# A hybrid attention and mLSTM step: the fourth head's scan on the projection's PSUM banks, run three blocks ahead, and a small DMA scratch

## The chip, the cores and the metric

The kernel runs on one core of one Trainium2 chip. The metric is the time of one execution on the device, in microseconds (us). Before the change, three runs gave 1586.22, 1588.04 and 1590.58 us; their median is 1588.04 us. The profile is one further execution, recorded by the hardware.

The engines are named as in the profile: PE is TensorE (matmuls), PEld its weight loads, DVE is VectorE, ACT is ScalarE, POOL is GpSimd, and SP is the engine that starts most DMAs. Each engine works through its own instructions strictly in the order of its queue. `L137` is line 137 of the kernel's source.

## The reference

One layer of a transformer-like step for 128 context tokens and 1024 latent tokens, D = 1024. Attention heads and mLSTM heads read one input projection and share one output projection, and a SwiGLU FFN follows. In short:

```python
h = rmsnorm(x, norm1_w) * (1 + sc1) + sh1                # sh1 .. g2 come from silu(cond) @ w_ada
aq, ak, av, mq, mk, mv, mo, mg = split(h @ w_in)
aq, ak = rope(rmsnorm(aq, q_norm_w)), rope(rmsnorm(ak, k_norm_w))   # rotary on latent tokens only
attn_o = softmax(aq @ keys.T / 8) @ vals                 # 8 query heads of 64, 2 key heads
hm = mlstm_bidir(mq, mk / sqrt(128), mv, gates)          # 4 heads of 128, forward and backward
hm = rmsnorm(hm) * sigmoid(mo)
x = x + g1 * (concat(attn_o, hm) @ w_out)
h2 = rmsnorm(x, norm2_w) * (1 + sc2) + sh2
x = x + g2 * swiglu(h2, w_gu, w_down)
# mlstm_scan, for one chunk of 128 tokens:
log_d = where(mask, b[:, None] - b[None, :] + i[None, :], -inf)
s = (q @ k.T) * exp(log_d - m_t)
num = s @ v + inter * (q @ C)                            # C, n: the state before this chunk
den = s.sum(-1) + inter * (q @ n)
out = num / maximum(abs(den), exp(-m_t))
```

The outputs are the two token groups after the layer, the normed keys and values of the context tokens, and the context's final mLSTM states.

## The kernel before

The tokens are nine blocks of 128 (block 0 is the context), in three chunks of three blocks. The program is one large function. Python generators emit pieces of the different strands of work in turns (`weave`, `beside`, `chain`), and a scheduler of the framework then sets the order of each engine's queue from the order of emission, from priorities (`hot`) and from its own model of when operands and memory are ready. Tiles are taken from pools; a tile whose memory was used by another must wait until the last use of that one. So both the number of buffers and the place of a pool in memory shape the order.

The stages by time in the profile:

- 0 to 84 us: the modulation of the inputs (`features`, L500 to L511, which makes `full` on DVE in pool `p0`) and the projection for keys, values and gates.
- 84 to 185 us: the projection of the queries (`linear_tok`, groups of blocks (0,1), (2,3), (4), (5,6), (7,8)). Beside it run the gates' work (L600 to L655), part of the modulation's matmuls with `w_ada` (`ada_rest`, L423 and L341), and the norm and rotary embedding (`norm_rope`, L657 to L686): first of the keys, in three calls, then of each query group after its evacuation (L724). One such call is: square on ACT (L664), sum on DVE (L666), a reciprocal root in twelve small DVE instructions (L127 to L133), a product on POOL (L668), the rotary products on DVE (L679) and POOL (L685), the sum on DVE (L686). Its scratch tile `nr` has one buffer, so the calls pass one behind another. `kw`, `qw`, and the tables `cc` and `ss` for keys and for queries are loaded at L913 to L922 into pool `qp`.
- 185 to 469 us: heads 0 to 3 of the mLSTM. `head_project` (L739) projects a head and forms its states; `head_mlstm` (L821), the scan, runs one head behind. Attention's first chunk runs beside both. The pairs of weights of a head are made on ACT and DVE (L198, L218, L219, L222, L137) from `iraw`, which SP loads (L193).
- 469 to 536 us: the scan of the fourth head, with no projection left, interleaved with the last modulation piece (`ada`, two buffers), the first half of the output projection (`attn_out_first`, L1144 to L1146) and attention's second chunk.
- 536 to 600 us: the second half of the output projection, and the second norm. Then the FFN to the end.

In the scan, `weights(b)` makes for a block the product of queries and keys and the masked log weights in one PSUM bank `pd` (PE, L840 to L843), two exponentials `dt` (ACT, L846), and their product `sd` (DVE, L848). For each block the scan then forms `pm` (PE L863, queries by states), `it` (ACT L866), `pn` (PE L870, `sd` by values), `nu` (DVE L873 or L875) and, after the normaliser, `hm` (ACT L883, DVE L884), the outputs of the head, which are stored to `hm_d` when several blocks are complete (L895). Before, `weights` runs one block ahead. `pd`, `pm`, `pn`, the modulation's and output projection's tiles and attention's transposes all take turns in the three banks of `bank()` (tag "mm"); two more banks (tag "wi", `bankA()`) belong to the projection and lie idle while the fourth head is scanned, and three hold attention's scores.

Of the kernel before, what the change touches and what calls it, by code (L numbers as in the profile page):

```python
# [8 lines left out]
F32 = mybir.dt.float32  # L9
F32R = mybir.dt.float32r  # L10
F16 = mybir.dt.float16
BF16 = mybir.dt.bfloat16
# [7 lines left out]
P = 128  # L20
D = 1024
KD = D // P
NB = 9
# [5 lines left out]
NH = 4  # L29
# [11 lines left out]
CSB = 21  # L41
# [4 lines left out]
def hybrid_step(ctx: ExitStack, tc: tile.TileContext, I: dict, O: dict):  # L46
    nc = tc.nc
# [10 lines left out]
    def nm(s):  # L58
        uid[0] += 1
        return f"{s}_{uid[0]}"  # L60
# [42 lines left out]
    def bank():  # L103
        return psum["mm"].tile([P, 512], F32, name=nm("mm"), tag="mm")
# [13 lines left out]
    def bc(ap, axis, shape):  # L118
        return ap.unsqueeze(axis).to_broadcast(shape)

    def rsqrt(tp, ss, n, inv, cap=16, plus=EPS):

        v = tp.tile([P, cap], F32, name=nm("rv"), tag="rv", bufs=2)[:, :n]
        y = tp.tile([P, cap], F32, name=nm("ry"), tag="ry", bufs=2)[:, :n]
        t = tp.tile([P, cap], F32, name=nm("rt"), tag="rt", bufs=2)[:, :n]
        h = tp.tile([P, cap], I32, name=nm("rh"), tag="rh", bufs=2)[:, :n]
        dve.tensor_scalar(out=v, in0=ss, scalar1=inv, scalar2=plus, op0=ALU.mult, op1=ALU.add)  # L127
        dve.tensor_scalar(out=h, in0=v.bitcast(I32), scalar1=1, scalar2=None, op0=ALU.logical_shift_right)
        dve.tensor_scalar(out=y.bitcast(I32), in0=h, scalar1=-1, scalar2=0x5F3759DF, op0=ALU.mult, op1=ALU.add)
        for _ in range(3):  # L130
            dve.tensor_tensor(out=t, in0=y, in1=y, op=ALU.mult)
            dve.scalar_tensor_tensor(out=t, in0=t, scalar=-0.5, in1=v, op0=ALU.mult, op1=ALU.mult)
            dve.scalar_tensor_tensor(out=y, in0=t, scalar=1.5, in1=y, op0=ALU.add, op1=ALU.mult)  # L133
        return y
# [389 lines left out]
    es0.close()  # L524
    mlp = es1.enter_context(tc.tile_pool(name="mlp", bufs=1, reuse_waits="tile"))
    mwh = mlp.tile([P, 512], F32, name="mwh")
    for tag, shape, bufs, dt in (("cs", [P, P + 1], CSB, F32), ("c0f", [P, P + 1], 2, F32), ("c0b", [P, P + 1], 1, F32), ("hm", [P, NB, P], 1, F32), ("ssh", [P, NB], 1, F32), ("nu", [P, 2, P + 1], 2, F32),
                                 ("it", [P, 2, P + 1], 1, F32), ("dn", [P, 2], 3, F32), ("jkh", [P, P], 1, BF16), ("sd", [P, 2, P], 2, F32),
                                 ("dt", [P, 2, P], 2, F32), ("so", [P, P], 9, F32), ("va", [P, P + 1], 9, F32), ("kT", [P, P], 9, F32),
                                 ("th", [P, P], 1, F32), ("qTm", [P, CT], 2 * NCH, F32), ("wv", [P, 2, P + 1], 2, F32), ("kt", [P, P], 2, F32)):  # L530
        mlp.tile(shape, dt, name=f"lay_{tag}", tag=tag, bufs=bufs)

# [204 lines left out]
    def qcol(i, d, b, h):  # L737
        c = d * 64 + b * 4 + h
        return QT[:, i, c : c + 1]  # L739
# [85 lines left out]
    def head_mlstm(h, st):  # L825

        blocks, states = st["b"], st["s"]
        for b in range(NBL, 1, -1):
            col = 64 + b * 4 + h
            dve.scalar_tensor_tensor(out=st["raw"][b], in0=states[1, b], scalar=decb[:, col : col + 1], in1=st["raw"][b],  # L830
                                     op0=ALU.mult, op1=ALU.add)
            states[1, b - 1] = st["raw"][b]
        hm = mlp.tile([P, NB, P], F32, name=nm("hm"), tag="hm", bufs=1)
        ssh = mlp.tile([P, NB], F32, name=nm("ssh"), tag="ssh", bufs=1)
        ends = {2: 0, 5: 3, 8: 6} if h == NH - 1 else {8: 0}

        def weights(b):
            qTb = st["q"][b // CB][:, b % CB * P : (b % CB + 1) * P]
            pd = bank()
            mm(pd[:, 0:P], blocks[b][0], qTb, start=True, stop=True)  # L840
# [3 lines left out]
            dt = mlp.tile([P, 2, P], F32, name=nm("dt"), tag="dt", bufs=2)  # L844
            for d in range(2):
                act(dt[:, d], pd[:, (d + 1) * P : (d + 2) * P], AF.Exp, bias=qcol(0, d, b, h))  # L846
            sd = mlp.tile([P, 2, P], F32, name=nm("sd"), tag="sd", bufs=2)
            dve.tensor_tensor(out=sd, in0=bc(pd[:, 0:P], 1, [P, 2, P]), in1=dt, op=ALU.mult)  # L848
            return qTb, sd

        ahead = [weights(0)]
        yield
        for b in range(NB):
            qTb, sd = ahead.pop(0)
            _, va, so = blocks[b]
            nu = mlp.tile([P, 2, P + 1], F32, name=nm("nu"), tag="nu", bufs=2)
            if b + 1 < NB:
                ahead.append(weights(b + 1))
            yield
            if b > 0:  # L860
                pm = bank()
                for d in range(2):
                    mm(pm[:, d * 256 : d * 256 + P + 1], qTb, states[d, b], start=True, stop=True)  # L863
                it = mlp.tile([P, 2, P + 1], F32, name=nm("it"), tag="it", bufs=1)
                for d in range(2):
                    act(it[:, d], pm[:, d * 256 : d * 256 + P + 1], AF.Copy, scale=qcol(2, d, b, h))  # L866
            yield
            pn = bank()
            for d in range(2):
                mm(pn[:, d * 256 : d * 256 + P + 1], sd[:, d], va, start=True, stop=True)  # L870
# [12 lines left out]
            act(hm[:, b, :], nu[:, 0, 0:P], AF.Copy, scale=dn[:, 0:1])  # L883
# [12 lines left out]
            yield  # L896
# [648 lines left out]
```

## Time and profile before

| | |
|---|---|
| runs, median of 3 | 1588.04 us (1586.22 to 1590.58) |
| the profiled execution, span | 1590.3 us |
| PE busy in it | 1494.7 us (94%) |
| DVE, ACT, POOL busy | 1027.2, 768.8, 267.4 us |
| PE busy, 125 to 185 us | 48.72 of 60 us |
| PE busy, 469 to 536 us | 52.78 of 67 us |
| PE busy, 600 to 1590 us | 969.91 of 990 us |

The profiled execution is one of its own, 2.3 us above the median of the runs. An engine's busy time says how much it does; what sets the end is read from the waits: for each wait of PE the profile names the instruction that ended it. Such a view is an inference from semaphores, and a wait for two things is put down to the later one. PEclk is the share of the full clock that TensorE was granted in a stretch.

### The profile page before, as it was taken

How to read it: one execution, taken by the hardware profiler on the slowest of the kernel's cores; microseconds unless marked ns; L12 is line 12 of the kernel's file. 1: busy time of each engine (PE TensorE's matmuls, PEld its weight loads, DVE VectorE, ACT ScalarE, POOL GpSimd, SP SyncE). 2: the span in 40 equal slices, each digit the busy share in tenths (PEclk: the TensorE clock that was granted, in tenths of full speed). 3: DMA queues.
4: the chain of work that ended last, by engine and by line, in shares of the span. 5: the costliest groups of instructions: out<-in, count | busy, mean ns of one | idle time of the engine just before them, and what ended most of it. 6: DMA issues, size and time to landing. Idle time of an engine off the chain costs nothing.

```text
span 1590.3 us, 23425 instructions
## 1 busy us (share of the span) xinstructions
PE 1494.7 (94%) x8539; PEld 1249.4 (79%) x8539; DVE 1027.2 (65%) x2025; ACT 768.8 (48%) x1409; POOL 267.4 (17%) x357
## 2 busy tenths in 40 slices
PE   6799799999988679999999999999999999999996
PEld 3544467666766467888999999999898989999995
DVE  4778645755757576667654667877875575554555
ACT  4854365846656354535433435555552443323332
POOL 0023342332332243100110001000010101001111
PEclk9899899999999899999999999999999999999998
DMA  9474322432547746957754547968774445544441
GB/s 358 160 200 140 94 75 36 103 77 52 117 113 179 237 103 149 221 158 176 173 158 129 159 127 230 198 154 198 165 173 126 153 133 178 155 121 137 146 144 53
DMA packets 387881, 236.91 MB, mean 149 GB/s; under 512 B 170198, under 2 KB 346790, under 8 KB 387766
## 3 DMA queue, kind: packets, MB, share of 16 engines
q1 hardware_dynamic: 385110, 231.84, 54.0%
q10 hardware_dynamic: 2656, 3.58, 1.1%
q8 instruction: 67, 1.10, 0.3%
q14 instruction: 48, 0.39, 0.1%
HBM read 183.79 MB, written 13.26 MB: 124 GB/s over the span
## 4 chain that ended last, share of the span: by engine, by line
PE 75%; DVE 9%; DMA 8%; ACT 4%; issue 2%; SPq 1%; POOL 1%; ACTq 0%; DVEq 0%; POOLq 0%
PE mm L1313 11%; PE mm L1314 11%; PE mm L1312 11%; PE mm L1112 5%; PE mm L1113 5%; PE mm L1114 5%; PE S L1032 4%; PE wi L485 3%; PE wi L483 3%; PE wi L484 3%; PE mm L1144 1%; PE mm L1145 1%; DMA aw<-in_w_ada_dram 1%; PE po L1057 1%; PE po L1056 1%
## 5 line engine op out<-in xcount | busy, mean ns | idle before, releaser
L152 ACT CAST whi<-raw 128x1024 fp32r<-128x1024 f32 (+1 forms) x216 | 221.8, 1027 | 413.0 <-PE mm L1313 151.5
L137 DVE TENSOR_TENSOR wlo<-raw,whi 128x1024 fp32r<-128x1024 f32 (+1 forms) x216 | 260.5, 1206 | 203.8 <-ACT whi L152 203.2
L1313 PE MATMUL mm<-aTl,whi 128*128 128x384 f32 x1056 | 355.9, 337 | 2.7 <-DVE aTl L137 2.7
L1314 PE MATMUL mm<-aTh,wlo 128*128 128x384 f32 x1056 | 354.3, 335 | 0.0
L1312 PE MATMUL mm<-aTh,whi 128*128 128x384 f32 x1056 | 353.2, 336 | 0.0
L137 POOL TENSOR_TENSOR hl<-tn,hl 128x384 fp32r<-128x384 f32 x66 | 85.5, 1295 | 839.5 <-ACT hl L1335 721.3
L1313 PEld LDWEIGHTS mm<-aTl,whi 128*128 128x128 f32 x1056 | 198.5, 188 | 3.9 <-DVE aTl L137 3.3
L1312 PEld LDWEIGHTS mm<-aTh,whi 128*128 128x128 f32 x1056 | 198.1, 188 | 0.6
L1314 PEld LDWEIGHTS mm<-aTh,wlo 128*128 128x128 f32 x1056 | 198.4, 188 | 0.0
L1113 PE MATMUL mm<-wlo,hl 128*128 128x512 f32 x372 | 145.5, 392 | 0.0
L1112 PE MATMUL mm<-whi,hl 128*128 128x512 f32 x372 | 144.1, 392 | 0.0
L1114 PE MATMUL mm<-whi,hl 128*128 128x512 f32 x372 | 143.2, 392 | 0.0
L483 PE MATMUL wi<-ipair,hT 128*128 128x384 f16 (+2 forms) x408 | 136.2, 337 | 1.8 <-ACT hT L507 1.2
L484 PE MATMUL wi<-ipair,hT 128*128 128x384 f16 (+2 forms) x408 | 136.4, 337 | 0.0
L485 PE MATMUL wi<-ipair,hT 128*128 128x384 f16 (+2 forms) x408 | 132.5, 337 | 1.0 <-DVE hT L137 1.0
L1039 DVE SCALAR_TENSOR_TENSOR pl<-pr,st,ph 128x1152 f16<-128x1152 f32 (+1 forms) x72 | 93.8, 1303 | 33.8 <-ACT ph L1038 33.7
L1034 DVE TENSOR_REDUCE st<-S 128x1 f32<-128x1152 f32 (+1 forms) x72 | 88.9, 1235 | 14.6 <-PE S L1032 14.1
L1032 PE MATMUL S<-kst,qT 128*128 128x384 f32 (+1 forms) x400 | 87.6, 350 | 9.8 <-ACT pr L1035 5.6
L1035 ACT ACTIVATE pr<-S,st 128x1152 f32<-128x1152 f32 (+1 forms) x72 | 81.3, 1129 | 29.6 <-DVE st L1034 25.6
L1038 ACT ACTIVATE ph<-pr,st 128x1152 f16<-128x1152 f32 (+1 forms) x72 | 83.8, 1165 | 23.2 <-DVE st L1037 6.7
L1101 DVE TENSOR_TENSOR t<-mm,gl 128x512 f32<-128x512 f32 x102 | 68.9, 685 | 28.1 <-DMA gl<-g_d 10.2
L1032 PEld LDWEIGHTS S<-kst,qT 128*128 128x128 f32 x400 | 70.6, 191 | 14.7 <-ACT pr L1035 7.0
(366 smaller groups left out, 2539.7 us busy)
## 6 DMA issues: line engine op xcount, KB each, us to landing
raw<-in_w_gu_dram SPq DMA_DIRECT2D x132, 512.0 KB
raw<-in_w_down_dram SPq DMA_DIRECT2D x60, 512.0 KB
a<-in_w_ada_dram SPq DMA_DIRECT2D x24, 512.0 KB
gl<-g_d SPq DMA_DIRECT2D x36, 256.0 KB
aw<-in_w_ada_dram SPq DMA_DIRECT2D x16, 512.0 KB
iraw<-in_w_in_dram SPq DMA_DIRECT2D x32, 256.0 KB
raw<-in_w_out_dram SPq DMA_DIRECT2D x12, 512.0 KB
x<-in_x_sample_dram SPq DMA_DIRECT2D x11, 512.0 KB
```

The source lines that it names most:

```text
L137: (dve if eng == "dve" else pool).tensor_tensor(out=out, in0=full, in1=hi, op=ALU.subtract)
L152: nc.scalar.copy(hi[:, :n], raw[:, :n])
L483: mm(ps[:, :n], ah, wh[:, k % 2, c0 : c0 + n], start=(k == 0), stop=False)
L484: mm(ps[:, :n], ah, wl[:, k % 2, c0 : c0 + n], start=False, stop=False)
L485: mm(ps[:, :n], al, wh[:, k % 2, c0 : c0 + n], start=False, stop=(k == KD - 1))
L1032: mm(S[:, n, 0:w], qT[:, h, :], kst[kv][:, t, c0 + n * w : c0 + (n + 1) * w], start=(t == 0), stop=(t == 1))
L1112: mm(ps, ah, wh[:, k % 2, :], start=(k == 0), stop=False)
L1113: mm(ps, ah, wl[:, k % 2, :], start=False, stop=False)
L1114: mm(ps, al, wh[:, k % 2, :], start=False, stop=(k == nk - 1))
L1312: mm(ps, wh[:, k, :], th[:, k, :], start=(k == 0), stop=False)
L1313: mm(ps, wh[:, k, :], tl[:, k, :], start=False, stop=False)
L1314: mm(ps, wl[:, k, :], th[:, k, :], start=False, stop=(k == KD - 1))
```

## The change

Three things, all in the diff:

1. In the scan of the fourth head alone (`alone`), `pm` and `pn` are taken from the projection's two banks (`wide = bankA`), and `weights` runs three blocks ahead in place of one (`depth = 3`).
2. More buffers for all heads: `hm` and `ssh` two in place of one, `nu` four for two, `it` three for one, `sd` and `dt` four for two. Together these are some 12.9 KB more in each partition.
3. The scratch that the program sets aside for dynamic DMAs, at the lowest addresses of each partition, is 256 bytes in place of 16384. All pools lie lower by the difference.

```diff
-    ... ("hm", [P, NB, P], 1, F32), ("ssh", [P, NB], 1, F32), ("nu", [P, 2, P + 1], 2, F32),
-        ("it", [P, 2, P + 1], 1, F32), ..., ("sd", [P, 2, P], 2, F32), ("dt", [P, 2, P], 2, F32), ...
+    ... ("hm", [P, NB, P], 2, F32), ("ssh", [P, NB], 2, F32), ("nu", [P, 2, P + 1], 4, F32),
+        ("it", [P, 2, P + 1], 3, F32), ..., ("sd", [P, 2, P], 4, F32), ("dt", [P, 2, P], 4, F32), ...
...
-        ends = {2: 0, 5: 3, 8: 6} if h == NH - 1 else {8: 0}
+        alone = h == NH - 1
+        ends = {2: 0, 5: 3, 8: 6} if alone else {8: 0}
+        depth = 3 if alone else 1
+        wide = bankA if alone else bank
...
-        ahead = [weights(0)]
+        ahead = [weights(b) for b in range(depth)]
...
-            if b + 1 < NB:
-                ahead.append(weights(b + 1))
+            if b + depth < NB:
+                ahead.append(weights(b + depth))
...
-                pm = bank()
+                pm = wide()
...
-            pn = bank()
+            pn = wide()
...
-    nc = _bacc.Bacc("TRN2", target_bir_lowering=False, num_devices=1)
+    nc = _bacc.Bacc("TRN2", target_bir_lowering=False, num_devices=1, dynamic_dma_scratch_size=256)
```

The lines of the changed kernel are three further down from L836 on (L913 before is L916 now).

What this does to the order of the queues is seen at three places. First SP, the engine that starts the DMAs, during the first projection. Before, `row` is the last load of that strand, and the keys' and queries' norm weights and rotary tables come behind all the later loads and stores of that strand:

```order
L448 DMA row_932<-in_b_ada_dram 2x512
L695 DMA out_new_cache_v_dram<-vall 128x128
L423 DMA a_93_784<-in_w_ada_dram 128x4x256
...
L193 DMA iraw_1059<-in_w_in_dram 128x4x128 x2
L734 DMA mwh<-in_mlstm_norm_w_dram 128x512
L913 DMA kw<-in_k_norm_w_dram 128x64
L914 DMA qw<-in_q_norm_w_dram 128x64
L921 DMA cc_1028<-in_k_cos_dram 128x8x64
L922 DMA ss_1029<-in_k_sin_dram 128x8x64
L921 DMA cc_1035<-in_k_cos_dram 128x8x64
L922 DMA ss_1036<-in_k_sin_dram 128x8x64
```

Now:

```order
L448 DMA row_932<-in_b_ada_dram 2x512
L916 DMA kw<-in_k_norm_w_dram 128x64
L917 DMA qw<-in_q_norm_w_dram 128x64
L924 DMA cc_1028<-in_k_cos_dram 128x8x64
L925 DMA ss_1029<-in_k_sin_dram 128x8x64
L924 DMA cc_1035<-in_k_cos_dram 128x8x64
L925 DMA ss_1036<-in_k_sin_dram 128x8x64
L695 DMA out_new_cache_v_dram<-vall 128x128
L423 DMA a_93_784<-in_w_ada_dram 128x4x256
```

The six loads moved up past the store of the context's values and all the later loads of `w_ada`.

Second DVE, at the end of the query projection, where the weight pairs of head 0 (`ipair`) are made and attention's first queries (`qT`) are formed. `nr_213` and `qraw_1606` are the third query group, block (4); `nrs_1759` and `nr_230` are the fourth, blocks (5, 6). Before:

```order
L137 TENSOR_TENSOR ipair_1902<-iraw_1062,ipair_1902 128x1024
...
L679 TENSOR_TENSOR nr_213_1629<-qraw_1606,ss_1036 128x16x16 x2
...
L686 TENSOR_TENSOR qraw_1606<-qraw_1606,nr_213_1629 128x512
L666 TENSOR_REDUCE nrs_1759<-nr_224_1757 128x16
...
L137 TENSOR_TENSOR qT_1986<-mm_1987,qT_1986 64x4x128
...
L137 TENSOR_TENSOR qT_1986<-mm_1987,qT_1986 64x4x128
L679 TENSOR_TENSOR nr_230_1778<-qraw_1754,ss_1036 128x16x16 x4
```

Now:

```order
L679 TENSOR_TENSOR nr_213_1629<-qraw_1606,ss_1036 128x16x16 x2
L219 TENSOR_SCALAR ipair_1892<-iraw_1059,isc_1211,ipair_1892 128x1024
L686 TENSOR_TENSOR qraw_1606<-qraw_1606,nr_213_1629 128x512
L137 TENSOR_TENSOR ipair_1895<-iraw_1060,ipair_1895 128x1024
L666 TENSOR_REDUCE nrs_1759<-nr_224_1757 128x16
...
L137 TENSOR_TENSOR ipair_1902<-iraw_1062,ipair_1902 128x1024
L137 TENSOR_TENSOR qT_1986<-mm_1987,qT_1986 64x4x128
L679 TENSOR_TENSOR nr_230_1778<-qraw_1754,ss_1036 128x16x16 x4
L137 TENSOR_TENSOR qT_1986<-mm_1987,qT_1986 64x4x128
```

The query groups' norm stands more than a group further up against the making of the pairs, and the second `qT` is now behind the fourth group's rotary product.

Third PE, at the start of the fourth head's scan (`pd` is a group of three matmuls; `ip` is a piece of `w_ada`). Before:

```order
L843 MATMUL mm_5728<-NM_105,selb 128x256
L840 MATMUL mm_5738<-qT_4749,kT_5074 128x128
...
L843 MATMUL mm_5738<-NM_105,selb 128x256
L870 MATMUL mm_5757<-va_4967,sd_5735 128x129 x2
L341 MATMUL mm_5765<-ip_5712,gta 32x256 x4
L341 MATMUL mm_5765<-ip_5711,gta 32x256 x4
L840 MATMUL mm_5776<-qT_4749,kT_5168 128x128
```

Now:

```order
L846 MATMUL mm_5728<-NM_105,selb 128x256
L843 MATMUL mm_5737<-qT_4749,kT_5074 128x128
...
L846 MATMUL mm_5737<-NM_105,selb 128x256
L843 MATMUL mm_5746<-qT_4749,kT_5168 128x128
...
L846 MATMUL mm_5746<-NM_105,selb 128x256
L843 MATMUL mm_5756<-qT_4820,kT_5260 128x128
...
L846 MATMUL mm_5756<-NM_105,selb 128x256
L873 MATMUL wi_5775<-va_4967,sd_5735 128x129 x2
L866 MATMUL wi_5807<-c_904_4690,qT_4749 128x129
L341 MATMUL mm_5783<-ip_5712,gta 32x256 x4
```

Four groups of weights stand ahead of the first product with the values, in place of two, and that product is in a bank of the projection (`wi`).

More of the change, by code (lines that the diff above doesn't have):

```diff
@@ L526, in hybrid_step @@
     mwh = mlp.tile([P, 512], F32, name="mwh")
-    for tag, shape, bufs, dt in (("cs", [P, P + 1], CSB, F32), ("c0f", [P, P + 1], 2, F32), ("c0b", [P, P + 1], 1, F32), ("hm", [P, NB, P], 1, F32), ("ssh", [P, NB], 1, F32), ("nu", [P, 2, P + 1], 2, F32),
-                                 ("it", [P, 2, P + 1], 1, F32), ("dn", [P, 2], 3, F32), ("jkh", [P, P], 1, BF16), ("sd", [P, 2, P], 2, F32),
-                                 ("dt", [P, 2, P], 2, F32), ("so", [P, P], 9, F32), ("va", [P, P + 1], 9, F32), ("kT", [P, P], 9, F32),
+    for tag, shape, bufs, dt in (("cs", [P, P + 1], CSB, F32), ("c0f", [P, P + 1], 2, F32), ("c0b", [P, P + 1], 1, F32), ("hm", [P, NB, P], 2, F32), ("ssh", [P, NB], 2, F32), ("nu", [P, 2, P + 1], 4, F32),
+                                 ("it", [P, 2, P + 1], 3, F32), ("dn", [P, 2], 3, F32), ("jkh", [P, P], 1, BF16), ("sd", [P, 2, P], 4, F32),
+                                 ("dt", [P, 2, P], 4, F32), ("so", [P, P], 9, F32), ("va", [P, P + 1], 9, F32), ("kT", [P, P], 9, F32),
                                  ("th", [P, P], 1, F32), ("qTm", [P, CT], 2 * NCH, F32), ("wv", [P, 2, P + 1], 2, F32), ("kt", [P, P], 2, F32)):
@@ L832, in head_mlstm @@
             states[1, b - 1] = st["raw"][b]
-        hm = mlp.tile([P, NB, P], F32, name=nm("hm"), tag="hm", bufs=1)
-        ssh = mlp.tile([P, NB], F32, name=nm("ssh"), tag="ssh", bufs=1)
-        ends = {2: 0, 5: 3, 8: 6} if h == NH - 1 else {8: 0}
+        hm = mlp.tile([P, NB, P], F32, name=nm("hm"), tag="hm", bufs=2)
+        ssh = mlp.tile([P, NB], F32, name=nm("ssh"), tag="ssh", bufs=2)
+        alone = h == NH - 1
+        ends = {2: 0, 5: 3, 8: 6} if alone else {8: 0}
+        depth = 3 if alone else 1
+        wide = bankA if alone else bank
         def weights(b):
```

8 lines of the change are left out of this document (4 added, 4 removed).

## The prediction

> **What bounds the kernel now.** I read the page's head first, then the busy times by stretch, then TensorE's waits inside the two stretches that the change touches, and last the chain of waits there. The head of the page:
>
> ```profile
> span 1590.3 us, 23425 instructions
> PE 1494.7 (94%) x8539; PEld 1249.4 (79%) x8539; DVE 1027.2 (65%) x2025; ACT 768.8 (48%) x1409; POOL 267.4 (17%) x357
> ```
>
> TensorE (PE) is busy 94% of the span, so a gain must come from the 95.6 us in which it is not, or from its clock. The windows show where those lie. Their columns are: stretch, length, busy time (with counts) of PE, its weight loads, DVE, ACT and POOL, then the granted clock, DMA share and GB/s.
>
> ```profile
> 50.00:70.00 20.00, 18.66 (x154) 14.65 (x152) 18.32 (x60) 16.27 (x42) 0.00 (x0) 0.90 0.03 9
> 70.00:84.00 14.00, 9.59 (x91) 4.72 (x84) 9.41 (x17) 9.29 (x15) 0.09 (x1) 0.90 0.80 254
> 84.00:125.00 41.00, 41.00 (x250) 20.81 (x248) 29.89 (x104) 20.28 (x42) 11.75 (x13) 0.95 0.71 197
> 125.00:160.00 35.00, 32.93 (x212) 15.75 (x210) 33.76 (x98) 15.22 (x25) 12.47 (x7) 1.00 0.37 120
> 160.00:185.00 25.00, 15.79 (x66) 9.50 (x67) 16.06 (x44) 12.46 (x26) 6.37 (x4) 0.73 0.42 127
> 185.00:469.00 284.00, 277.20 (x1805) 198.12 (x1803) 161.48 (x429) 178.05 (x502) 92.64 (x211) 0.99 0.38 80
> 469.00:536.00 67.00, 52.78 (x321) 39.18 (x320) 52.60 (x152) 34.67 (x90) 21.43 (x23) 0.95 0.60 150
> 536.00:600.00 64.00, 47.09 (x210) 36.12 (x211) 40.83 (x90) 29.08 (x46) 20.93 (x16) 0.89 0.63 182
> 600.00:1590.00 990.00, 969.91 (x5284) 894.90 (x5283) 638.97 (x938) 426.46 (x565) 100.67 (x78) 0.99 0.59 157
> ```
>
> The FFN (600 to 1590) is bound by PE, and there the change only exchanges a few neighbouring rows of its order. The heads (185 to 469) leave 284.00 − 277.20 = 6.8 us. Two stretches have room: the end of the query projection (125 to 185: 2.07 + 9.21 = 11.3 us idle, and a clock of 0.73 in its last 25 us), and the fourth head's scan (469 to 536: 14.2 us idle).
>
> **Part 1: the scratch.** All DMAs in the trace's list of issues are SP's or ACT's, none POOL's, so the smaller scratch costs no instruction anything. What it does is move every tile down by about 16 KB a partition, and by that an overlap goes. Before, the memory of the rotary tables `cc`, `ss` and of `kw`, `qw` lies where the last features of the first projection (`full`, L508) lie, so their loads wait for those. After, the first projection's pool ends below them. SP's order, shown with the change, has the result: the six loads go right behind `row` of L448. The trace of before, on SP, POOL and ACT:
>
> ```profile
> 44.82 0.60 SPq L448 DMA_DIRECT2D row<-in_b_ada_dram  x1
> 59.38 0.38 SPq L695 DMA_DIRECT2D out_new_cache_v_dram<-vall  x1
> 95.36 2.32 SPq L922 DMA_DIRECT2D ss<-in_k_sin_dram  x1
> 98.22 1.27 POOL L923 TENSOR_TENSOR cc<-cc,kw 128x512 f32<-128x512 f32 x1 [14.21 <-DMA cc<-in_k_cos_dram]
> 113.61 0.63 ACT L664 ACTIVATE nr<-kall 128x512 f32<-128x512 f32 x1 [0.32 <-DVE kall L686]
> ```
>
> Now they would go at 45.4 instead of 90 to 98, into a gap of SP of 14 us, and land in the stretch 50 to 70 where the DMA share is 0.03. What follows is the norm and rotary chain. `nr` has one buffer, so K's two large groups and the five query groups pass through it one at a time, each behind the one before. The chain of waits shows one link:
>
> ```profile
> 118.60 1.05 POOL kall L668
> 119.68 1.18 DVE nr L679 x8
> 121.00 1.28 POOL kall L685
> 122.30 0.69 DVE kall L686
> 123.09 1.07 ACT nr L664
> ...
> 174.76 1.23 DVE nrs L666
> ```
>
> The query groups begin at 123.09, when K is through, and the fourth of the five is at 174.76. PE's waits between 84 and 185 (who waited, for what; total, times, longest):
>
> ```profile
> PE S L1032 <- DVE qT L137: 4.1, 1, 4.1
> PE mm L347 <- ACT part L441: 3.8, 1, 3.8
> PE mm L116 <- DVE scale L333: 1.8, 1, 1.8
> PE mm L116 <- ACT qraw L724: 1.5, 1, 1.5
> ```
>
> All four stand behind norm instructions in the queues of ACT and DVE (`part` behind an L664 that waited for L686, `qT` behind the small instructions of the fourth group). They sum to 11.2 us, the idle time above. With the tables there early, K's first group runs among the last features. Before, it took from the tables' product (98.22) to the second group's L664 (113.61); so all behind it may come up to 15.4 us sooner, more than the four waits together.
>
> The bounds: nothing gained, or all idle time and the lost clock of 160 to 185 (15.79 × 0.27 = 4.3 us), together −15.6. I do not take it whole, for two reasons. DVE has 33.76 of 35 us to do from 125 to 160, so part of the wait is its work and only what moves ahead of 125 helps. And the new order brings a wait of its own: on ACT the L198 on `iraw_1929` now stands ahead of the L218 that makes `ipair_1899`. Before:
>
> ```profile
> 156.77 1.14 ACT L218 ACTIVATE ipair<-iraw,isc 128x1024 f16<-128x1024 f32 x1
> 161.54 1.00 SPq L193 DMA_DIRECT2D iraw<-in_w_in_dram  x2
> 164.49 0.63 ACT L198 ACTIVATE jkw<-iraw 128x512 bf16<-128x512 f32 x1
> ```
>
> That load needs the buffer of the first pair, so about 3 us from issue to L198 (161.54 to 164.49) come ahead of the third pair; PE has the first two pairs' 24 matmuls meanwhile. Behind the L198 stand the L218, the next L198 and L724, and PE waits for them with head 0's projection. I put 3 us of PE's waiting on this and some 4 us on DVE's own work: −15.6 + 3 + 4 = **−8.5**.
>
> [...]
>
> **Part 2: the fourth head's scan.** PE's order has now four groups of weights (`pd`, L840 to L843) ahead of the first `pn` (L870), and `pm`, `pn` are in the two banks that the projection left. PE's waits of 469 to 536 before, the largest five:
>
> ```profile
> PE mm L870 <- DVE sd L848: 3.7, 2, 3.0
> PE mm L341 <- DMA ip<-in_w_ada_dram: 2.1, 2, 1.4
> PE mm L870 <- ACT it L866: 1.5, 1, 1.5
> PE po L1056 <- DVE ir L451: 1.4, 1, 1.4
> PE mm L840 <- ACT it L866: 1.4, 2, 1.0
> ```
>
> The first is the weights' latency (ACT's exponentials, then DVE's product), which running ahead hides, except that the fourth group waits for the first of three banks: its `sd` is then what is late. The third and fifth are the shared banks and go. The fourth has `S` matmuls put ahead of it now. The second is a load into two buffers that nothing here makes earlier; it stays. So 3.7 + 1.5 + 1.4 + 1.4 = 8.0 us are within reach. With two `hm` buffers this goes too:
>
> ```profile
> 484.31 0.70 ACT L883 ACTIVATE hm<-nu,dn 128x128 f32<-128x128 f32 x2 [2.55 <-DMA hm_d<-hm]
> ```
>
> The bounds: nothing, since DVE has 52.60 us to do in order and the chain from state to state goes through it; or all idle time, −14.2. No instruction is added. Of the 8.0 I take five eighths, since the bank of the fourth group and DVE give some back: **−5**.
>
> **Part 3: the other heads and the tail.** Two buffers of `hm` and `ssh`, more of `nu`, `it`, `sd`, `dt` for heads 0 to 2: bounds 0 and −6.8 (all idle of 185 to 469); PE is busy 98% there and its order keeps but for short exchanges of neighbours, so **−0.5**. From 536 on PE waits for what the memory brings:
>
> ```profile
> PE mm L116 <- DMA t<-hm_d: 6.4, 1, 6.4
> ```
>
> An earlier end of the scan moves this as a whole: the store and the output weights are asked for as much earlier. **0**, with up to +6 given back if the loads of the weights, not the scan, end last there.
>
> **The sum**: −8.5 − 5 − 0.5 + 0 = −14 us against 1590.3, the profiled span; that execution is 2.3 us above the runs' median of 1588.04, so the median goes to **1574**.
>
> **Rivals.** *Only the place of the stall moves* in the early part: PE waits for the weight pairs behind ACT's L198, or for the second `qT`, which in DVE's order now stands behind the L679 of the group (5, 6). For: both are in the order. Against: the pairs' load is short. Early −3, the rest as above: 1579.5. *The scan gives nothing*, because DVE's 52.60 of 67 us and the `ip` loads pace it, or the tail gives it back: −9, 1579. *Both parts in full*, −14 and −10: 1564. *The change does not do what it says*: the tables land early but the groups are paced by their own PE work, and the scan by its states: −1, 1587.
>
> *Slower*: VectorE's order in the first projection. K's first group now stands among the features (L679 between `full_850` and `full_854`, L686 ahead of `full_862`), where PE has only 9.59 of 14 us, and waits for POOL there with the features behind it. One group costs DVE its L666 (0.6 us, half of the 1.23 above for half the columns), 1.18, 0.69 and twelve small ones, and the waits for POOL of 1.05 and 1.28. The rows for the small ones and for the second `qT`:
>
> ```profile
> 164.17 0.17 DVE L128 TENSOR_SCALAR rh<-rv 128x8 int32<-128x8 int32 x1
> 179.33 1.90 POOL L668 TENSOR_TENSOR qraw<-qraw,ry 128x1024 f32<-128x1024 f32 x1 [7.00 <-DVE ry L133]
> 181.27 1.43 DVE L679 TENSOR_TENSOR nr<-qraw,ss 128x256 f32<-128x256 f32 x4 [0.93 <-POOL qraw L668]
> ```
>
> 0.6 + 1.18 + 0.69 + 12 × 0.17 + 2.33 = 6.8 us on the features, and the second `qT` 1.90 + 1.43 = 3.3 us later behind the larger group, with no gain in the query chain: +10.1, less 5 for the scan, +5: 1593. It decides if the tables' products come after the features' own inputs (after about 79). For it: DVE has 9.41 of 14 us there. Against it: the tables would be ready by 60, and PE waits there for weights, under which such work hides.
>
> *The clock in the scan.* If PE stops more often and briefly as it changes banks, the granted clock of 0.95 could fall to the 0.73 that 160 to 185 shows behind its waits: 52.78 × 0.95 / 0.73 − 52.78 = +15.9 us less the 14.2 of idle time that would be filled, so about +2 in place of −5: 1581. Against it: the waits themselves get fewer. [...]
>
> **How the numbers follow.** The forecast 1574 has 0.45 (its own range 1567 to 1581); the stall that moves 0.14; the scan without gain 0.13; both in full 0.10; the clock 0.04; no effect 0.05; slower 0.09. A change of 0.3%, 4.8 us, is about what this measurement tells from none: faster is below 1583.3, slower above 1592.8. The forecast, both in full, and most of the three cases at 1579 to 1581 are faster: 0.45 + 0.10 + 0.24 = 0.79. Within: no effect, what is left of those three, and a little of the slower case: 0.11. Slower 0.10, with all that I have not seen. The range leaves out the slower case above and half of the full one below: 1563 to 1587.
>
> **What would show it.** Right: the loads of L921 and L922 (three lines further down now) issued near 45; the second K group's L664 by 100; PE's waits of 84 to 185 below 4 us, with a clock near 1.0 up to head 0; head 0's first `S` some 8 us earlier; in the scan no wait of `pn` for `sd` over 1 us after the start, none for `it`, no ACT wait for the store of `hm`, and its stretch about 62 us long. Wrong: PE waits for L219 or L222 of the pairs of head 0; DVE idle at L679 or L686 ahead of L508; the scan as long as before with DVE busy all through; or a longer wait for `hm_d` or the output weights behind it. The forecast fails altogether if the first 84 us grow.

## The result and the profile after

| | median, us | runs | ratio to before (95%) |
|---|---|---|---|
| before | 1588.42 | 1586.22 to 1590.58 | |
| changed | 1574.19 | 1572.71 to 1574.52 | 0.9911 (0.9897 to 0.9925) |

The row of before has four runs, the three named above and one of 1588.80 us. The ratios in this document are those of the record, worked out from all runs of a pair of kernels; they can differ in the fourth place from the quotient of the two medians. The change takes 14.2 us off. The head of the page of the changed kernel:

```profile
span 1572.3 us, 23397 instructions
PE 1487.7 (95%) x8539; PEld 1247.3 (79%) x8539; DVE 1022.9 (65%) x2025; ACT 771.8 (49%) x1409; POOL 271.4 (17%) x357
```

The two profiled executions differ by 18.0 us, 3.8 more than the medians. The run that was profiled here took 1574.08 us for a span of 1572.3, so some 1.8 us lie outside a span; the profiled execution of before, with a span of 1590.3, was thus about 4 us above its median, and not 2.3.

Where the time went is read by instructions that both kernels have. The table is from the timelines of ACT and PE. `th` is ACT's L760 (nine in each head), the last `hm` ACT's L883 of the scan's last block (L886 in the changed kernel). The last landmark is PE's first product with `w_down` (L1112, now L1115); the expectations call it the FFN's first matmul, though the FFN's products with `w_gu` (L1312, now L1315) begin some 45 us sooner.

| profiled, us | before | changed | difference |
|---|---|---|---|
| first `th` of head 0 | 193.60 | 183.20 | −10.4 |
| last `th` of head 3 | 467.76 | 455.29 | −12.5 |
| last `hm` of the scan | 529.98 | 512.94 | −17.0 |
| first product with `w_down` | 677.60 | 659.55 | −18.1 |
| end | 1590.3 | 1572.3 | −18.0 |

The early part gives 10.4 us, from the last `th` to the first product with `w_down` another 5.6, all behind it nothing. The 2.1 us between the first and the last `th` may be that one execution of before: it took 274.2 us for them, the changed kernel 272.1, and the versions below 268.9 to 271.3, the one without any change of the heads (270.2) among them.

**The early part.** SP, ACT and DVE in the timeline of the changed kernel (start, duration, instruction, and in brackets the idle time before it and what ended it):

```profile
44.71 0.40 SPq L448 DMA_DIRECT2D row<-in_b_ada_dram  x1
46.01 0.74 SPq L916 DMA_DIRECT2D kw<-in_k_norm_w_dram  x1
52.22 1.15 SPq L925 DMA_DIRECT2D ss<-in_k_sin_dram  x1
...
68.23 0.66 ACT L664 ACTIVATE nr<-kall 128x512 f32<-128x512 f32 x1
97.18 0.65 ACT L664 ACTIVATE nr<-kall 128x512 f32<-128x512 f32 x1
...
83.20 1.23 DVE L508 TENSOR_SCALAR full<-x,scale,shift 128x384 f32<-128x384 f32 x2
84.45 0.69 DVE L686 TENSOR_TENSOR kall<-kall,nr 128x512 f32<-128x512 f32 x1
85.06 1.25 DVE L508 TENSOR_SCALAR full<-x,scale,shift 128x384 f32<-128x384 f32 x2
```

The six loads now go at 46.0 to 53.4. The keys' second group starts its norm at 97.18 in place of 113.61. What it costs shows too: the keys' L686 stands between the last features, and the last L508 ends at 86.31; before it was at 83.77:

```profile
81.37 2.40 DVE L508 TENSOR_SCALAR full<-x,scale,shift 128x384 f32<-128x384 f32 x4
```

PE's waits between 84 and 185 now, and the windows of that part (columns as in the prediction):

```profile
PE mm L116 <- DVE ry L133: 3.6, 1, 3.6
PE wi L808 <- DVE QT L654: 2.0, 1, 2.0
```

```profile
84.00:125.00 41.00, 40.85 (x259) 19.65 (x257) 28.91 (x90) 20.28 (x41) 7.45 (x7) 1.00 0.58 172
125.00:160.00 35.00, 31.36 (x197) 15.53 (x195) 31.39 (x102) 17.25 (x30) 9.65 (x6) 0.95 0.51 162
160.00:185.00 25.00, 23.02 (x137) 14.00 (x135) 16.41 (x41) 11.52 (x26) 7.82 (x7) 0.93 0.31 93
```

Two waits, 5.6 us together, stand in place of four, 11.2 together, and the clock of 160 to 185 is 0.93 in place of 0.73. PE's busy time multiplied by its clock, summed over the three stretches, is 92.05 us in place of 83.41: by this estimate some 8.6 of the 10.4 us are found here.

**The scan and behind it.** PE's waits from the last `th` to the last `hm` (455 to 513), all of them:

```profile
PE mm L785 <- POOL wv L783: 2.1, 1, 2.1
PE po L1059 <- DVE ir L451: 1.6, 1, 1.6
PE mm L1147 <- DVE sd L851: 1.2, 1, 1.2
PE mm L843 <- DVE sd L851: 0.8, 1, 0.8
```

The waits for `sd`, `it` and the `ip` loads, 8.7 us before (3.7, 1.5 and 1.4, 2.1), are 2.0 now. Over the same stretch of before (467.8 to 530.4) all waits sum to 11.9 us, and to 5.7 now; the wait for `ir` is still there (1.4 before), and the one for `wv` is not among those of before. But behind the scan, between attention's last products and the second half of the output projection, PE waits longer. SP and PE there, changed, then before:

```profile
514.53 7.88 SPq L151 DMA_DIRECT2D raw<-in_w_out_dram  x3
522.46 0.47 SPq L1161 DMA_DIRECT2D t<-hm_d  x1
...
526.75 1.12 PE L116 MATMUL mm<-ident,t 128*128 128x128 f32 x4 [9.40 <-DMA t<-hm_d]
```

```profile
534.29 1.11 SPq L151 DMA_DIRECT2D raw<-in_w_out_dram  x2
535.45 0.47 SPq L1158 DMA_DIRECT2D t<-hm_d  x1
```

Three weight pieces stand ahead of `t` in SP's queue where there were two, there are two `raw` buffers, and the third load holds the queue from 515 to 522. The wait for `hm_d` is 9.4 us; before it was 6.4. The 3 us are not a loss of the tail as a whole, though: from the last `hm` to the first product with `w_down` it is 146.6 us now and was 147.6 before (the table above).

### The profile page after: what moved, and what is told of

The parts are those of the page before. It is cut to its first block, busy times and chain, and to the rows that moved or that the text cites. A ratio compares the mean times of both kernels' runs of the same rounds, so it can differ in the third digit from the quotient of the medians.

```text
span 1572.3 us, 23397 instructions
## 1 busy us (share of the span) xinstructions
PE 1487.7 (95%) x8539; PEld 1247.3 (79%) x8539; DVE 1022.9 (65%) x2025; ACT 771.8 (49%) x1409; POOL 271.4 (17%) x357
## 4 chain that ended last, share of the span: by engine, by line
PE 77%; DVE 11%; DMA 5%; ACT 4%; issue 2%; SPq 0%; POOL 0%; ACTq 0%; DVEq 0%; POOLq 0%
PE mm L1316 11%; PE mm L1317 11%; PE mm L1315 11%; PE mm L1115 5%; PE mm L1116 5%; PE mm L1117 5%; PE S L1035 3%; PE wi L483 3%; PE wi L485 3%; PE wi L484 3%; PE mm L116 2%; PE mm L1147 1%; PE mm L1148 1%; PE mm L1149 1%; PE po L1060 1%
## 5 line engine op out<-in xcount | busy, mean ns | idle before, releaser
L1315 PE MATMUL mm<-aTh,whi 128*128 128x384 f32 x1056 | 353.3, 336 | 0.0
L1315 PEld LDWEIGHTS mm<-aTh,whi 128*128 128x128 f32 x1056 | 198.1, 188 | 0.6
L1115 PE MATMUL mm<-whi,hl 128*128 128x512 f32 x372 | 144.3, 392 | 0.0
L1117 PEld LDWEIGHTS mm<-whi,hl 128*128 128x128 f32 x372 | 69.9, 188 | 14.2
```

What stands on the lines that cost most here:

```text
L1115: mm(ps, ah, wh[:, k % 2, :], start=(k == 0), stop=False)
L1117: mm(ps, al, wh[:, k % 2, :], start=False, stop=(k == nk - 1))
L1315: mm(ps, wh[:, k, :], th[:, k, :], start=(k == 0), stop=False)
```

## The experiments

Times are medians of 4 to 11 runs beside the kernel before on the same chip. The last two columns are from the profiles: the times from the last `th` of head 3 to the last `hm` and to the first product with `w_down`, and the first `th` of head 0. A profile is of one execution, and not always of a median one: with all but the early order it is 4.7 us below the median, with three `raw` buffers 3.3 and with the shared banks 2.5 below, with only the buffers 2.4 above. Differences of 2 or 3 us in these columns tell little.

| run | median | before | ratio (95%) | th to hm, th to `w_down` | first `th` |
|---|---|---|---|---|---|
| before | | | | 62.2, 209.8 | 193.6 |
| changed | 1574.19 | 1588.42 | 0.9911 (0.9897 to 0.9925) | 57.6, 204.3 | 183.2 |
| small scratch alone | 1577.09 | 1587.47 | 0.9936 (0.9922 to 0.9949) | 64.8, 210.9 | 182.2 |
| all but the early order | 1583.84 | 1587.47 | 0.9972 (0.9958 to 0.9986) | 58.0, 204.0 | 191.5 |
| one block ahead | 1572.27 | 1587.47 | 0.9905 (0.989 to 0.992) | 56.5, 206.7 | 182.3 |
| two blocks ahead | 1580.90 | 1587.15 | 0.9964 (0.9951 to 0.9976) | 52.0, 215.4 | 181.6 |
| shared banks | 1574.67 | 1587.15 | 0.9916 (0.9901 to 0.9932) | 59.2, 207.6 | 181.1 |
| one `hm` buffer | 1574.68 | 1587.15 | 0.9915 (0.99 to 0.993) | 57.6, 205.2 | 183.8 |
| old `nu`, `it`, `sd`, `dt` | 1578.32 | 1587.15 | 0.994 (0.9925 to 0.9954) | 53.4, 211.3 | 184.9 |
| only these buffers | 1574.69 | 1588.17 | 0.9924 (0.9909 to 0.9939) | 61.9, 209.4 | 183.0 |
| `t` loaded by ACT | 1572.12 | 1587.47 | 0.9902 (0.9887 to 0.9918) | 57.7, 205.9 | 182.6 |
| two ahead, weights first | 1577.53 | 1589.58 | 0.9925 (0.9908 to 0.9941) | 53.0, 210.7 | 182.5 |
| the same, three `raw` | 1576.92 | 1589.58 | 0.9924 (0.9909 to 0.9939) | 50.1, 208.4 | 180.3 |
| old buffers, weights first | 1571.59 | 1588.17 | 0.9908 (0.9886 to 0.993) | 53.4, 203.7 | 183.3 |

### The small scratch alone

```diff
-    nc = _bacc.Bacc("TRN2", target_bir_lowering=False, num_devices=1)
+    nc = _bacc.Bacc("TRN2", target_bir_lowering=False, num_devices=1, dynamic_dma_scratch_size=256)
```

> The kernel of before with the DMA scratch of 256 bytes and nothing else of the change. Theory (two gains that add; the small scratch takes the rotary tables' memory away from the first projection's): the early part goes as in the changed kernel, head 0's first th near 183 us in place of 193.6 (-10.4), the scan and the tail as before, so 1588.4 - 10 = about 1578, with 1576 to 1580 allowed. Rival (the early gain is lost again at later waits, and the whole 14 us come from the scan): 1588. Second rival (the time is all the memory's, the scan's part gains nothing): 1574.

1577.09 against 1587.47, −10.4 us, and the first `th` at 182.2. The theory holds: the smaller scratch is worth most of the change. No DMA in the traces of before and of the changed kernel is started by POOL: all are SP's or ACT's.

### The changed kernel with the early order of before

```diff
     es0 = ExitStack()
+    pad = es0.enter_context(tc.tile_pool(name="pad", bufs=1, reuse_waits="tile"))
+    pad.tile([P, 4032], F32, name="pad")
     p0 = es0.enter_context(tc.tile_pool(name="p0", bufs=1, reuse_waits="tile"))
```

> The changed kernel with 15.75 KB of unused memory below pool p0 alone, so that the first projection's features lie where they lay before, over the rotary tables; all else of the change stays. Theory: the six loads wait until about 90 us again, head 0's first th is at 193.6 again, and the scan's gain stays: 1588.4 - 5 = about 1583.5, 1581 to 1586 allowed. Rival (the gain is all the scan's): 1574. Second rival (the small scratch helps by itself, not by the overlap): head 0 stays at 183 and the time at 1574.

1583.84 against 1587.47: −3.6 us, inside what was allowed. Only the place of one pool differs from the changed kernel, and the loads go where they went before, with PE's old waits behind them. SP, and PE's waits from 84 to 185, of this version (its lines are two further down than the changed kernel's):

```profile
89.06 0.43 SPq L918 DMA_DIRECT2D kw<-in_k_norm_w_dram  x1
```

```profile
PE S L1037 <- DVE qT L137: 5.0, 1, 5.0
PE mm L349 <- ACT part L443: 3.8, 1, 3.8
PE mm L116 <- DVE scale L335: 1.5, 1, 1.5
PE mm L116 <- ACT qraw L726: 1.4, 1, 1.4
```

So it is the overlap in memory, and not the small scratch by itself.

This sets right what is said above, that every pool lies lower: if all had moved by the same amount, no overlap could have changed. `p0` (L264) is laid from the lower end of the partition, while `qp`, the pool of the tables, is opened with `side="right"` (L913 before), from the other end. The scratch moves the first and, as the two runs imply, not the second. No view of the profile gives addresses.

The two runs sum to −14.0 us; the change gave −14.2.

### The scan's parts, one undone at a time

```diff
-        depth = 3 if alone else 1
+        depth = 1
```

> The changed kernel with the weights of the fourth head's scan one block ahead again (depth 1); the two banks for pm and pn, the buffers and the scratch stay. Theory (of the scan's gain the larger part is the latency of sd, 3.7 of 8.0 us of PE's waits): PE waits again some 3 us for sd at the scan's start, 1574.2 + 2.5 = about 1577. Rival (the banks alone give it, since pn's bank is what made PE wait): 1574, no wait of pn for sd over 1 us. Second rival (the scan is paced by DVE and the states): 1574 with waits only moved.

```diff
-        wide = bankA if alone else bank
+        wide = bank
```

> The changed kernel with pm and pn of the fourth head's scan in the three shared banks again; three blocks ahead, buffers and scratch stay. Theory (after the run with depth 1, which lost nothing: the banks are what the scan gained by): PE waits for it or nu by turns of the three banks again, 2 to 4 us in all, and the time is 1574.2 + 3 = about 1577. Rival (the second hm buffer and the other buffers gained it, the banks and the depth are worth nothing): 1574. Second rival (depth and banks each suffice, either alone gives the gain): 1574, with the waits of pn for sd below 1 us as well.

```diff
-        hm = mlp.tile([P, NB, P], F32, name=nm("hm"), tag="hm", bufs=2)
-        ssh = mlp.tile([P, NB], F32, name=nm("ssh"), tag="ssh", bufs=2)
+        hm = mlp.tile([P, NB, P], F32, name=nm("hm"), tag="hm", bufs=1)
+        ssh = mlp.tile([P, NB], F32, name=nm("ssh"), tag="ssh", bufs=1)
```

> The changed kernel with one buffer each for hm and ssh again (the freed memory is left unused, so that all other tiles keep their places). Theory (the wait of ACT for the store of the third head's hm, 2.55 us before, is off the path that sets the scan's end, since the scan has other work): 1574 to 1575, ACT waits some 2 us at the fourth head's first hm. Rival (this wait began the scan late, and is the larger part of its gain): 1577 to 1578, with the scan's first nu or hm instructions later by 2 to 5 us against the last th of the head.

None of the three lost anything that can be measured in the time: ratios 0.9905, 0.9916 and 0.9915 beside 0.9911. My theory fell for the first two (1577 was expected for each). With one block ahead PE has no wait for `sd` at all between the last `th` and the last `hm`, where 3 us were expected. With three ahead in the shared banks waits for `sd` and `it` come back, as expected, but the time does not follow them:

```profile
PE mm L843 <- DVE sd L851: 2.3, 1, 2.3
PE mm L873 <- ACT it L869: 1.4, 2, 0.7
PE mm L873 <- DVE sd L851: 0.7, 1, 0.7
```

So the two banks alone take the wait of `pn` (L873) for `sd` away, which is 3.1 us with only the buffers (below). Running ahead alone takes it to 0.7 and brings 2.3 at the fourth group of weights (L843). In these two profiles the stretch from the last `th` to the first product with `w_down` is 2.4 and 3.3 us longer than in the changed kernel, near the loss expected, and the heads before it are 2.2 and 3.2 us shorter. One execution of each can't tell whether that is chance. My theory held for the third part, where ACT waits again for the store of the third head's `hm` and the end does not move:

```profile
473.02 0.69 ACT L886 ACTIVATE hm<-nu,dn 128x128 f32<-128x128 f32 x2 [2.01 <-DMA hm_d<-hm]
```

### The buffers of the scan

```diff
-            dt = mlp.tile([P, 2, P], F32, name=nm("dt"), tag="dt", bufs=4)
+            dt = mlp.tile([P, 2, P], F32, name=nm("dt"), tag="dt", bufs=2)
...
-            sd = mlp.tile([P, 2, P], F32, name=nm("sd"), tag="sd", bufs=4)
+            sd = mlp.tile([P, 2, P], F32, name=nm("sd"), tag="sd", bufs=2)
...
-            nu = mlp.tile([P, 2, P + 1], F32, name=nm("nu"), tag="nu", bufs=4)
+            nu = mlp.tile([P, 2, P + 1], F32, name=nm("nu"), tag="nu", bufs=2)
...
-                it = mlp.tile([P, 2, P + 1], F32, name=nm("it"), tag="it", bufs=3)
+                it = mlp.tile([P, 2, P + 1], F32, name=nm("it"), tag="it", bufs=1)
```

> The changed kernel with the old counts of buffers for nu (2), it (1), sd and dt (2), the freed memory left unused; the two banks, three blocks ahead and two hm buffers stay. Theory: with two sd and dt buffers the weights can run only two blocks ahead whatever the program says, and it holds one block; 1574 to 1576, near the run with depth 1. Rival (the buffers are what the other parts stand on): the scan goes as before, 1578.

1578.32, as the rival said, and the scan's whole gain gone. But the rival's reason is wrong: this scan ends 53.4 us after the last `th`, 4 us sooner than in the changed kernel, and what is lost is lost behind it. There PE waits 4.46 and 5.77 us for `whi`, the split output weights. The runs below show how.

### Two blocks ahead

```diff
-        depth = 3 if alone else 1
+        depth = 2 if alone else 1
```

> The changed kernel with the weights two blocks ahead in place of three. In its order the first load of hm_d behind the scan stands ahead of the output weights' loads on SP. Theory (three blocks ahead put that load behind the third weight piece, which gives back 2 us or so at the tail; the depth itself is worth nothing): about 1572, as with one block ahead, and PE's wait for hm_d below 6 us. Rival (the tail is paced by the output weights, whatever stands first): 1574.

1580.90: this version, with the load of `hm_d` first, is slower by 6.7 us, not faster. I had looked at the wrong load. The scan is again quick (52.0 us from `th` to `hm`), but SP and PE behind it, in this version:

```profile
516.42 1.69 SPq L1161 DMA_DIRECT2D t<-hm_d  x1
...
518.65 0.94 SPq L151 DMA_DIRECT2D raw<-in_w_out_dram  x2
519.63 1.18 SPq L1139 DMA_DIRECT2D gl<-g_d  x2
...
527.29 1.61 SPq L151 DMA_DIRECT2D raw<-in_w_out_dram  x2
...
517.16 0.40 PE L1059 MATMUL po<-phT,vs 128*128 128x256 f16 x1 [9.64 <-DVE oT L1064]
525.75 0.80 PE L1147 MATMUL mm<-whi,mx 128*128 128x512 f32 x1 [3.88 <-ACT whi L152]
...
537.72 0.80 PE L1147 MATMUL mm<-whi,mx 128*128 128x512 f32 x1 [5.71 <-ACT whi L152]
```

The output weights are asked for at 518.65 and 527.29, 68.2 and 76.8 us after the last `th` (450.5); in the changed kernel the first three are in the queue 59.2 us after it. PE waits twice for `whi`, which ACT makes from them. The 9.64 us are an in-order queue as well: `oT` needs `ol` (L1062), which on ACT stands behind the store of the scan's outputs, and that waits for POOL:

```profile
513.49 2.36 ACTq L898 DMA_DIRECT2D hm_d<-hm  x2
515.89 0.47 ACT L1062 ACTIVATE ol<-po,vsc 64x256 f32<-64x256 f32 x1 [9.08 <-POOL hm L896]
```

### The tail's order alone

In the first, on top of two blocks ahead, and in the last, on top of the old buffers, the four weight pieces come first; the middle one adds a third `raw` buffer, and raises the load of `t` as well:

```diff
-        ahead = load_hm(0)
-        load_x1(0)
-        ws = out_pieces(1)
+        with hot(300):
+            ws = out_pieces(1)
+        ahead = load_hm(0)
+        load_x1(0)
```

> Two blocks ahead, and the four loads of the output weights behind the scan asked for first (their pieces stand ahead of the loads of hm_d and x in the program, with a higher priority). Theory (the 6.7 us that two blocks ahead lost against three are the order of SP's queue at the tail: t, x, the gates and the context's row stood ahead of the third and fourth weight piece, and PE waited 3.9 and 5.7 us for whi): the waits for whi go below 2 us together and the time is 1571 to 1574. Rival (two blocks ahead hurt the scan itself): 1579 to 1581 with the same order as the changed kernel at the tail.

> The same with three raw buffers in place of two and the first load of hm_d right behind the weights', so that the third weight piece waits for no buffer. Theory (the tail is paced by the output weights): another 2 to 4 us off, 1568 to 1571, with PE's longest wait between the scan and the norm below 6 us. Rival (the tail is paced by the last attention product and by the norm behind it): the same as the run before it, and the FFN unchanged at about 912.8 us from its first matmul to the end.

> The changed kernel with the old counts of buffers for nu, it, sd and dt, as in an earlier run, and now the four loads of the output weights behind the scan asked for first. Theory (that run lost 4 us by the order of SP's queue at the tail, as two blocks ahead did, PE waiting 4.5 and 5.8 us for whi, and not in the scan, which ended 53.4 us after the head's last th, earlier than in the changed kernel's 57.6): the waits for whi fall below 2 us together and the ratio to before is 0.991 to 0.992, about 1574 to 1576. Rival (the old buffers hold the scan back): 1578 again, with the wait moved to oT or hm_d.

With two blocks ahead, the waits for `whi` fell to 1.0 us and the ratio from 0.9964 to 0.9925, 3.9 parts in a thousand, about 6 us; the two intervals do not meet. It did not reach the 1571 to 1574 that I expected (1577.5, where the kernel before ran at 1589.6). The wait for `oT` stayed, which may be why; no run took it away. In the profile of this version:

```profile
520.02 0.39 PE L1059 MATMUL po<-phT,vs 128*128 128x256 f16 x1 [9.62 <-DVE oT L1064]
...
535.47 0.51 PE L1147 MATMUL mm<-whi,mx 128*128 128x512 f32 x1 [0.99 <-ACT whi L152]
```

The third `raw` buffer brought nothing more (0.9924): the rival holds there. With the old buffers the weights first brought the ratio from 0.994 to 0.9908, about as expected, and no wait of PE for `whi` is left. The intervals (0.9925 to 0.9954 and 0.9886 to 0.993) just touch. So SP's order accounts for the loss of the buffers' run, and nothing shows that the old buffers hold the scan back.

### Only the buffers

The changed kernel with depth 1, shared banks and one `hm` buffer.

> The changed kernel with depth 1, pm and pn in the shared banks and one buffer for hm and ssh again: of the scan's part only the added buffers of nu, it, sd and dt stay, with the small scratch. Theory (undoing depth, banks or hm alone lost nothing, undoing these buffers lost all: so they are what the scan's gain needs): ratio to before 0.991, about 1574. Rival (each of the parts alone is worth nothing, the scan gains only by two of them together): ratio 0.9936, about 1577 to 1578, as with the small scratch alone.

0.9924 (0.9909 to 0.9939) lies between the two values expected and tells neither from the other. The scan itself shows no gain (61.9 us from `th` to `hm`, PE waits again 3.1 us for `sd` and 3.0 for `it`). One rival was not run: every version with buffers taken away keeps their 12.9 KB laid out, so no run tells whether part of the scan's gain comes from where the pools lie then.

### The load behind the scan

```diff
-            dma(hm, hm_d[b // CB][b % CB * P : (b % CB + 1) * P, :])
+            (nc.scalar.dma_start if b == 0 else dma)(hm, hm_d[b // CB][b % CB * P : (b % CB + 1) * P, :])
```

> The changed kernel with one DMA moved: the first load of hm_d behind the scan (t, block 0) is started by ACT and not by SP, where it stands behind the third load of the output weights, which waits for one of two raw buffers (514.5 to 522.4 us). Theory (part of the scan's gain is given back there: PE waits 9.4 us for this load in place of 6.4 before): t lands by 521, PE starts when the first two weight pieces are split, near 523 in place of 526.75, so 3 to 4 us less: about 1571. Rival (the third weight piece or the norm behind it ends last anyway): PE starts earlier and waits as much for the third piece, 1574.

1572.12 beside the changed kernel's 1574.19, at ratios of 0.9902 and 0.9911, whose intervals overlap: the sign is the expected one, the size is not settled. The timelines of PE and ACT in this version show why it is less than 4:

```profile
520.36 1.11 PE L116 MATMUL mm<-ident,t 128*128 128x128 f32 x4 [8.30 <-DMA t<-hm_d]
525.93 0.80 PE L1147 MATMUL mm<-whi,mx 128*128 128x512 f32 x1 [4.46 <-ACT mx L1184]
...
517.50 1.04 ACT L152 CAST whi<-raw 128x1024 fp32r<-128x1024 f32 x1 [0.21 <-DMA raw<-in_w_out_dram]
517.57 0.34 ACTq L1161 DMA_DIRECT2D t<-hm_d  x1
524.22 1.04 ACT L152 CAST whi<-raw 128x1024 fp32r<-128x1024 f32 x1 [5.67 <-DMA raw<-in_w_out_dram]
525.29 0.59 ACT L1184 CAST mx<-mm 128x512 fp32r<-128x512 f32 x1
```

`t` comes earlier: PE starts on it 68.9 us after the last `th`, in place of 71.5 in the changed kernel. But `mx`, which needs it, stands on ACT behind the third `whi`, and that waits for the third weight piece, so PE waits another 4.46 us, as the rival said.

## Why the prediction was right, and where it was not

**The time** was forecast at 1574 and came at 1574.19, from terms of −8.5, −5 and −0.5. That it came within 0.2 us is luck: part 1 measured 1.9 us more than its term and part 2 1.4 us less, and the two misses nearly cancel.

**Part 1, −8.5:** right in mechanism, somewhat small in size (its own sum, −15.6 + 3 + 4, gives −8.6). The scratch alone measured −10.4 us, the padded version shows that the overlap is the cause. That "every tile" moves down is not so, as said with the padded version. Of the two things that I took off the bound of −15.6, the wait behind L198 is there: ACT waits 1.77 us for the load, and the third pair and `QT` on DVE follow it; PE waits 2.0 us where 3 was allowed.

```profile
159.81 0.63 ACT L198 ACTIVATE jkw<-iraw 128x512 bf16<-128x512 f32 x1 [1.77 <-DMA iraw<-in_w_in_dram]
...
165.01 0.32 PE L808 MATMUL wi<-hT,ipair 128*128 128x384 f16 x1 [1.98 <-DVE QT L654]
```

The L218 behind it begins at 161.19, about when PE's last query matmul (160.94, 0.38 us), which reads a pair, ends. If L218 needed that pair's buffer, the L198 alone cost less than that; no run took it away. DVE's own work left 3.6 us of waiting for `ry`. The waits are 5.6 us, not below 4, and the clock is 0.93 to 0.95, not 1.0. The slower rival's place is real too: the features end 2.5 us later (86.31 for 83.77), where 6.8 was its price, and the earlier norm outweighs it.

**Part 2, −5:** the size was near (−3.6 by the padded version, 5.6 between the profiles' `th` and `w_down`), and PE's waits for `sd` and `it` fell as named. Three steps failed. "The first is the weights' latency (ACT's exponentials, then DVE's product), which running ahead hides": with one block ahead and the two banks PE has no wait for `sd`, so nothing had to be hidden; with three ahead and the shared banks 0.7 us are left, and 2.3 come at the fourth group, the case that the prediction excepted. "[I]t stays", of the load of `ip`: its 2.1 us are gone. And the fourth wait, for `ir`, did not go: 1.6 us for 1.4. The shared banks do bring waits back, as said, but the time with one block ahead, with the shared banks, or with one `hm` buffer is the same. No single one of these three carries the gain, so what I priced by parts can't be added by parts; what carries it stays open.

**Part 3, 0 with up to +6 given back at the tail:** the wait for `hm_d` grew by 3.0 us, one of the signs named for being wrong, and the tail as a whole came out 1.0 us shorter, so the term of 0 holds. What I had wrong is the reason, that the tail moves "as a whole". The order of SP's loads there, which came out differently in several of the versions, was worth some 6 us with two blocks ahead: a scan that ends 5.6 us sooner (52.0 for 57.6) gave a kernel 6.7 us slower. In this the change was lucky, since its order has the weights first.

**The −0.5 of the other heads** can't be told from nothing; the small scratch alone, with the old buffers, took 270.2 us from the first to the last `th`, and the changed kernel 272.1.

**The base** was misread: the profiled execution of before was some 4 us above its median. That did no harm, since the sum is a difference, taken off the median in the end.

A version that beats the changed kernel clearly was not found. Loading `t` from ACT, one block ahead, and the old buffers with the weights first came out 1.9 to 2.6 us lower by medians, with ratios that overlap its own.

## What to carry to other kernels

Before costing a change of sizes, see which pools come to lie on which: a tile placed over a late user of its memory has its load held back with no line of code that says so (`kw` was asked for at 89.06 us with the padding, at 46.01 without), and 16 KB of scratch, without which the kernel runs as well, decided 10.4 us here. Pools laid from the two ends of a partition need looking at together. When a stage ends earlier, look at the queue that brings the next stage's operands, and at the place of each load in it: what is saved in front of it is kept only if the loads that the next stage needs first are also first (two blocks ahead gave a ratio of 0.9964, and 0.9925 with the weights first). And where several edits each remove a wait of the same chain, undo them one at a time; the gain may belong to none of them alone.

## What was not expected of the hardware

The same POOL product took twice as long once in an execution: 2.87 us at 81.54, 1.27 at 109.82, in the changed kernel. Before, both took 1.27 us (at 109.80 and 121.00).

```profile
81.54 2.87 POOL L685 TENSOR_TENSOR kall<-kall,cc 128x512 f32<-128x512 f32 x1 [4.05 <-DVE nr L679]
...
109.82 1.27 POOL L685 TENSOR_TENSOR kall<-kall,cc 128x512 f32<-128x512 f32 x1 [4.48 <-DVE nr L679]
...
81.33 1.94 DVE L137 TENSOR_TENSOR hT<-full,hT 128x384 f16<-128x384 f32 x4
```

DVE ran four subtractions there, from 81.33 to 83.27; the slow product began at 81.54. It took 1.60 us longer than the later one, and 1.73 us of these subtractions lie behind its start. That the one comes from the other was not shown; no run here took them apart.

TensorE's granted clock was lower beside longer waits at the tail as well as in the early part (0.73 there before, 0.93 now, from 160 to 185). No run took waits and clock apart. In the version with two blocks ahead, the stretch from 505 to 560, with waits of 9.64, 3.88, 5.71 and 4.65 us, had a clock of 0.72. The changed kernel's from 510 to 565, with one of 9.40 and none other above 2.5, had 0.84:

```profile
505.00:560.00 55.00, 30.31 (x120) 23.34 (x119) 29.91 (x75) 18.03 (x28) 11.38 (x11) 0.72 0.66 214
```

```profile
510.00:565.00 55.00, 35.57 (x169) 26.87 (x166) 35.21 (x91) 24.10 (x40) 13.94 (x12) 0.84 0.70 210
```
